# Head 0's value weights, z sums, values' ends and output blocks of a hybrid attention layer put in another order

## The chip, the cores and the metric

The kernel runs on one core of one Trainium2 chip. The metric is the device time of one execution in microseconds (us), as a median over several runs. The core has a matrix engine (TensorE, PE in the profile; its weight loads are PEld), a vector engine (DVE), an activation engine (ACT), a slower general engine (GpSimd, POOL) and a queue engine (SyncE, SP) that here issues most of the DMAs. They run side by side and wait for each other through semaphores. The profile also names SPq, the queue engine's issuing of DMAs.

## The reference

One layer of a decoder over 512 tokens plus 16 learned meta tokens, width 1024. A forgetting-attention branch (FoX, 8 heads of 128) and a matrix-memory branch (mLSTM, 4 heads, values of 512, queries and keys of 256 behind a causal convolution) run on the same normalised input, are gated and merged, and pass one output projection.

```python
h = rms_norm(x, g_pre); z = h @ w_in
(fq, fk, fv, ff, fz, mqk, mv, mi, mf, mo, mz, ga, gb) = split(z)
oa = forgetting_attention(fq, fk, fv, log_sigmoid(ff + b_fox_f))
ya = (oa * silu(fz)) @ w_a
mq, mk = split(silu(causal_conv(mqk, conv_w, conv_b)))
hb = mlstm_scan(mq * 256**-0.5, mk, mv, mi + b_i, log_sigmoid(mf + b_f))
hb = rms_norm(sigmoid(mo) * hb, g_head)      # per head
yb = (hb * silu(mz)) @ w_b
merged = sigmoid(ga) * ya + sigmoid(gb) * yb
out = x + rms_norm(merged @ w_o, g_post)     # meta tokens removed
```

All of it is float32. The kernel keeps that accuracy by splitting an operand into a high and a low part and doing three matmuls for each product (`mm3`: high x high, high x low, low x high).

## The kernel before

**Splits.** A weight chunk is loaded by SP into one of 4 raw buffers (`wload`, 512 KB), its high part is a copy on ACT, and its low part is a subtraction on DVE (`wsplit`, L142 and L144; `split`, L250 and L252). High and low parts have 4 buffers each, so a new split waits until TensorE is done with an older one.

**Products with seven multiplications.** Some projections (`mz`, `mo` of heads 1 to 3, values of heads 1 to 3, and most of the attention's) use a two by two scheme with seven block products instead of eight (`st_products`: X, Y, Z, W, Y, X, Z in that order, 12 matmuls each per unit). It needs sums of weight blocks on DVE: `st_narrow` forms them as L263, L264 (for the second and third product, s3 and s1) and L269, L270 (for the last two, s2 and s4), each followed by a split. `b` and `d` in a split's name (wz00b, wz00d) are these sums' splits, `a` and `c` the plain blocks'. The products' ends are snapshots on ACT and sums in the result's PSUM banks on DVE (L333, L334, L336).

**Order.** The four mLSTM heads come first. For each: `conv_part` for q and k (projection, then vector steps L732 to L739), values, `mo`, `score_part`, `value_part` for the chunks 3 and 2, `mz_part(h, 0)`, `value_part` for the chunks 1 and 0, `mz_part(h, 1)`. Of head 0 the values' first half is made while the input is normalised; its second half has weights of its own (`v_chunk(0, 1)`, tile wv, product pv), and its `mo` is plain (`mo_plain`, four sigmoids at L779). Heads 1 to 3 make all values in `v_seven`. Then come four pairs of attention heads; `fv_part` makes their values with `v_seven` as well, and `prob_part` the logits `pl`.

**Scores.** `score_part` takes j = 0 to 4: a product in a bank `ps`, times the decay `w` on DVE (L765), a copy to the high part `wh` on ACT (L766), the low part `wl` on DVE (L768). The last one, j = 4, is that of the meta tokens and ends with L770. `value_part` multiplies these with the values: for a chunk c and a half u (bank pnb for u = 1, pna for u = 0) three matmuls for each j (L829, L830, L831), then one with the meta rows (L832).

**Who sets the order.** The instructions stand in the program as written, each engine runs its own in a fixed order, and that order is made by the framework's scheduler when the kernel is built: it goes by program order, but lets a later instruction go ahead where, by its own model of durations, the earlier one is not ready. `pin` keeps instructions in program order, and `behind(a, b)` adds an edge so that `a` comes after `b` without a wait of its own. PSUM has 8 banks (pool `pa`), and a bank is taken again when its last reader is done. Tiles with the tag "w" share one buffer: `z` of the convolutions, the decay `w` of the scores, and `so` of heads 1 to 3.

**POOL in head 0.** The gates' rows are packed on POOL (`mr` L666, `na` L672), and behind them stands the memset of the k convolution's `z` (L708), which ACT's copies into `z` (L724) wait for.

**Output.** `wo` is taken in three parts: columns 0 to 511 with all four token blocks in four banks, and then 256 columns twice, each for the four blocks one after the other, a bank half used. A block's end is a sum of squares on ACT (L1161), a product with the gain on DVE (L1162), and after the last part the root on POOL (L1184), the two final steps (L1187) and two DMAs.

Of the kernel before, what the change touches and what calls it, by code (L numbers as in the profile page):

```python
# [10 lines left out]
BF16 = mybir.dt.bfloat16  # L11
# [42 lines left out]
def tile_hybrid_block(ctx: ExitStack, tc: tile.TileContext, x, meta, norm_pre, norm_post, w_in, b_fox_f,  # L54
# [200 lines left out]

    def st_narrow(c0, name, into=None, late=None, first=None):

        (r0,), (r1,) = (wload(win, 512 * i, 4, c0, 256, f"{name}{i}")[0] for i in range(2))
        a, b = slice(0, P), slice(P, 2 * P)
        o = {"a11": split(r0[:, :, a], f"{name}a", ("whs", "wls"), mw, 1, into)}  # L260
        if first:
            behind(split.first, first)
        V.tensor_tensor(r0[:, :, a], r0[:, :, a], r0[:, :, b], ALU.add)  # L263
        V.tensor_tensor(r0[:, :, b], r0[:, :, b], r1[:, :, b], ALU.add)  # L264
        x, y = split(r0, f"{name}b")
        o["s3"], o["s1"] = (x[:, :, a], y[:, :, a]), (x[:, :, b], y[:, :, b])
        x, y = split(r1, f"{name}c")
        o["a12"], o["a22"] = (x[:, :, a], y[:, :, a]), (x[:, :, b], y[:, :, b])
        d = V.tensor_tensor(r1[:, :, b], r0[:, :, a], r1[:, :, b], ALU.add)  # L269
        V.tensor_tensor(r1[:, :, a], r1[:, :, a], r1[:, :, b], ALU.add)  # L270
        x, y = split(r1, f"{name}d")
        if late:
            behind(d, late[0])
            behind(split.first, late[1])
        o["s4"], o["s2"] = (x[:, :, a], y[:, :, a]), (x[:, :, b], y[:, :, b])
        return o
# [17 lines left out]

    def st_products(o, units, between=lambda i: None):

# [17 lines left out]
        def halves(bank):  # L314
            return bank.rearrange("p (s n) -> p s n", s=2)
# [145 lines left out]
    def v_seven(c0, name, v, snaps, q1):  # L461
# [18 lines left out]

        st_products(o, units, meta)
        for i in (1, 0):
            for m in range(2):
                pv = units[m][i].rearrange("p (s n) -> p s n", s=2)
                hi, lo = (t[:, :, i * 256:i * 256 + 256].rearrange("p (s m) n -> p m s n", m=2)[:, m]
                          for t in (vh, vl))
                S.activation(hi, pv, AF.Copy)
                V.tensor_tensor(lo, pv, f(hi), ALU.subtract)  # L488
        v_meta(vm[:, 0:MV], pm)
# [214 lines left out]

    def conv_part(h, which):
        w = w_first[which] if h == 0 else wsplit(conv_load(h, which))
# [10 lines left out]
        for m in range(2):  # L717
            mi = which * 8 + h * 2 + m
            ps = banks(f"pqk{which}{h}{m}", 2)
            proj_t_all(ps, w, m, tz)  # L720
            y = sb([P, L], F32, "y", f"y{which}{h}{m}", bufs=2)
            for u in range(2):
                c0 = tz + u * nz
                S.activation(z[:, m, 3 + c0:3 + c0 + nz], ps[u][:, 0:nz], AF.Copy)  # L724
                S.activation(y[:, c0:c0 + nz], ps[u][:, 0:nz], AF.Identity,  # L725
                             bias=gc[:, 64 + mi:65 + mi], scale=gc[:, 48 + mi:49 + mi])
            ys.append(y)
        for m in range(2):
            mi = which * 8 + h * 2 + m
# [12 lines left out]
    def score_part(h, q, k, w):  # L742
# [10 lines left out]
        for j in range(NCH + 1):  # L753
# [13 lines left out]
            if j < NCH:  # L767
                V.tensor_tensor(wl[:, o:o + n], w[:, o:o + n], f(wh[:, o:o + n]), ALU.subtract)  # L768
            else:
                V.tensor_tensor(wh[96:128, o:o + n], w[96:128, o:o + n], f(wh[96:128, o:o + n]), ALU.subtract)  # L770
        return wh, wl
# [26 lines left out]

    def st_unit(c0, name, room, into=None, late=None, first=None):

        ps = banks(f"p{name}", 2)
        st_unit.added = st_products(st_narrow(c0, f"w{name}", into, late, first),
                                    [(ps[0], ps[1], room.rearrange("p a (b n) -> p (a b) n", b=2), None)])
# [16 lines left out]
    def value_part(h, wpk, v, so, hts, chunks):  # L820
        wh, wl = wpk
        vh, vl, vm = v
        for c in chunks:
            pn = (psum1(f"pna{h}{c}"), psum1(f"pnb{h}{c}"))
            for u in (1, 0):
                o, n = u * 256, 256 + 2 * u
                for j in range(c + 1):
# [3 lines left out]
                    T.matmul(pn[u][:, 0:n], wl[:, s0:s0 + P], vh[:, j, o:o + n], start=False, stop=False)  # L831
                T.matmul(pn[u][:, 0:n], wh[0:MP, OFFM + c * P:OFFM + (c + 1) * P], vm[0:MP, o:o + n],  # L832
                         start=False, stop=True)
            r = line(wk, f"r{h}{c}", 1, tag="r", bufs=4)
# [54 lines left out]
    for h in range(MH):  # L889
        if pend is not None:  # L890
            bt = turn_part(*pend)
        q = conv_part(h, 0)
        if h == 0:
            w1 = v_chunk(0, 1)
        k = conv_part(h, 1)
# [4 lines left out]
        if h == 0:  # L900
            v = v0
            ps = banks("pv01", 2)
            for b in range(NCH):
                proj_n(ps, w1, b)
            v_end(0, v, 1, w1, ps)
            columns()
# [264 lines left out]
    for b in range(NCH):  # L1171
        out_end(pn[b], b, 0, 512, 0)
    for u in (2, 3):
        w = wchunk(wo, 0, KC, u * 256, 256, f"wo{u}")
        for b in range(NCH):
            ps = psum1(f"pout{u}{b}")
            for k in range(KC):
                mm3(ps[:, 0:256], mh_[k // 2][:, k % 2, b * P:(b + 1) * P], ml_[k // 2][:, k % 2, b * P:(b + 1) * P],
                    w[0](k, 0, 256), w[1](k, 0, 256), k == 0, k == KC - 1)
            out_end(ps[:, 0:256], b, u * 256, 256, u - 1)  # L1180
            if u == 3:
                rs = line(wk, f"ors{b}", 1, tag="rs", bufs=7)
                V.scalar_tensor_tensor(rs, oss[:, b, 2:3], 1.0 / DM, opre[:, b:b + 1], ALU.mult, ALU.add)
                G.tensor_tensor(rs, rs, mhalf, ALU.pow)  # L1184
                for i in range(2):
                    cs = slice(i * 512, i * 512 + 512)
                    V.scalar_tensor_tensor(og[:, b, cs], og[:, b, cs], rs, xr[b][:, cs], ALU.mult, ALU.add)  # L1187
                    nc.sync.dma_start(out2[b * P:(b + 1) * P, cs], og[:, b, cs])
# [28 lines left out]
```

## Time and profile before

| | |
|---|---|
| median of 3 runs | 928.46 us (928.32 to 929.09) |
| profiled execution | 927.63 us |
| its span, first to last instruction | 925.8 us |
| TensorE busy | 906.0 us, 98% |
| vector engine busy | 730.4 us, 79% |
| activation engine busy | 504.5 us, 54% |
| POOL busy | 117.5 us, 13% |
| mean granted TensorE clock | 0.999 |

A row of the timeline gives the start in us, the length in us, the engine, the line of the kernel, the operation, what it writes and reads, the shapes and a count; in brackets stands the engine's idle time before it and what ended that. A row of the waits gives who waited for whom, the sum in us, how often, and the longest. A row of the windows gives a stretch, its length, the busy times of PE, PEld, DVE, ACT and POOL with their numbers of instructions, the granted clock, and the DMAs' share and rate. Matmuls overlap: a 512-column matmul has a length of 0.39 us in the trace, and the next one starts 0.23 us after it.

### The profile page before, as it was taken

How to read it: one execution, taken by the hardware profiler on the slowest of the kernel's cores; microseconds unless marked ns; L12 is line 12 of the kernel's file. 1: busy time of each engine (PE TensorE's matmuls, PEld its weight loads, DVE VectorE, ACT ScalarE, POOL GpSimd, SP SyncE). 2: the span in 40 equal slices, each digit the busy share in tenths (PEclk: the TensorE clock that was granted, in tenths of full speed). 3: DMA queues.
4: the chain of work that ended last, by engine and by line, in shares of the span. 5: the costliest groups of instructions: out<-in, count | busy, mean ns of one | idle time of the engine just before them, and what ended most of it. 6: DMA issues, size and time to landing. Idle time of an engine off the chain costs nothing.

```text
span 925.8 us, 16722 instructions
## 1 busy us (share of the span) xinstructions
PE 906.0 (98%) x6744; PEld 858.4 (93%) x6744; DVE 730.4 (79%) x1196; ACT 504.5 (54%) x860; POOL 117.5 (13%) x168
## 2 busy tenths in 40 slices
PE   8999899999999999999999999999999999999997
PEld 6998799899998999999999989999999999988887
DVE  6889688579887598876898866997896997985534
ACT  5646556545665456664565525565755665863231
POOL 3052000100101000000100002221333121300000
PEclk9999999999999999999999999999999999999999
DMA  7313143123331333231242442344342333258402
GB/s 233 94 50 103 46 134 91 40 69 92 117 112 57 92 91 90 95 103 51 95 114 69 124 128 73 95 123 137 100 142 81 102 112 121 87 203 300 140 18 91
DMA packets 78664, 97.54 MB, mean 105 GB/s; under 512 B 5237, under 2 KB 66773, under 8 KB 78586
## 3 DMA queue, kind: packets, MB, share of 16 engines
q1 hardware_dynamic: 76520, 92.76, 32.5%
q0 software_dynamic: 576, 2.10, 0.6%
q10 hardware_dynamic: 1490, 1.61, 0.5%
q8 instruction: 53, 0.87, 0.4%
q14 instruction: 25, 0.20, 0.1%
HBM read 90.62 MB, written 5.83 MB: 104 GB/s over the span
## 4 chain that ended last, share of the span: by engine, by line
PE 66%; DVE 22%; ACT 5%; issue 3%; DMA 2%; POOL 1%; DVEq 0%; POOLq 0%; ACTq 0%
PE pyb L151 3%; PE pyb L150 3%; PE pyb L152 3%; PE pz L150 3%; PE pz L152 3%; PE pz L151 3%; PE pqk L150 3%; PE pqk L152 3%; PE pqk L151 3%; PE pv L152 2%; PE pv L150 2%; PE pv L151 2%; PE pfk L150 2%; PE pfk L152 2%; PE pfk L151 2%
## 5 line engine op out<-in xcount | busy, mean ns | idle before, releaser
L151 PE MATMUL pyb<-bl,wb_h 128*128 128x512 f32 x128 | 49.8, 389 | 0.0
L152 PE MATMUL pyb<-bh,wb_l 128*128 128x512 f32 x128 | 49.8, 389 | 0.0
L150 PE MATMUL pyb<-bh,wb_h 128*128 128x512 f32 x128 | 49.8, 389 | 0.0
L1016 POOL TENSOR_SCALAR pn<-lt,rsum 128x128 f32<-128x128 f32 x32 | 30.4, 952 | 127.6 <-DVE rsum L1014 127.5
L732 DVE SCALAR_TENSOR_TENSOR y<-z,gc,y 128x512 f32<-128x512 f32 (+1 forms) x48 | 35.9, 754 | 2.1 <-ACT y L725 1.4
L150 PE MATMUL pfk<-hh,wfk_h 128*128 128x264 f32 x128 | 36.4, 285 | 0.0
L150 PE MATMUL pqk<-hh,wq_h 128*128 128x258 f32 x128 | 36.4, 284 | 0.0
L150 PE MATMUL pqk<-hh,wk_h 128*128 128x264 f32 x128 | 36.3, 284 | 0.0
L151 PE MATMUL pfk<-hl,wfk_h 128*128 128x264 f32 x128 | 36.3, 283 | 0.0
L152 PE MATMUL pqk<-hh,wk_l 128*128 128x264 f32 x128 | 36.3, 283 | 0.0
L152 PE MATMUL pfk<-hh,wfk_l 128*128 128x264 f32 x128 | 36.3, 283 | 0.0
L151 PE MATMUL pqk<-hl,wk_h 128*128 128x264 f32 x128 | 36.2, 283 | 0.0
L152 PE MATMUL pqk<-hh,wq_l 128*128 128x258 f32 x128 | 36.0, 282 | 0.0
L151 PE MATMUL pqk<-hl,wq_h 128*128 128x258 f32 x128 | 36.0, 282 | 0.0
L849 POOL TENSOR_TENSOR mrs<-mss,mhalf 128x1 f32<-128x1 f32 x16 | 9.2, 575 | 191.1 <-DVE mss L847 188.2
L993 POOL TENSOR_TENSOR ab<-ab,mask_q 128x128 f32<-128x128 f32 x32 | 27.0, 874 | 49.5 <-DVE vl L488 34.8
L144 DVE TENSOR_TENSOR wo_l<-wo_r,wo_h 128x1024 fp32r<-128x1024 f32 x12 | 15.7, 1313 | 16.9 <-ACT wo_h L142 16.9
L152 PEld LDWEIGHTS pyb<-bh,wb_l 128*128 128x128 f32 x128 | 24.0, 188 | 5.0
L150 PEld LDWEIGHTS pyb<-bh,wb_h 128*128 128x128 f32 x128 | 24.0, 188 | 4.9
L151 PEld LDWEIGHTS pyb<-bl,wb_h 128*128 128x128 f32 x128 | 24.0, 188 | 4.8
L884 DVE TENSOR_TENSOR yb<-pyb,yb 128x512 f32<-128x512 f32 x24 | 16.5, 686 | 13.9 <-PE pyb L152 13.9
L142 ACT ACTIVATE wo_h<-wo_r 128x1024 fp32r<-128x1024 f32 x12 | 12.7, 1059 | 24.4 <-PE pya L151 13.2
(2206 smaller groups left out, 3961.2 us busy)
## 6 DMA issues: line engine op xcount, KB each, us to landing
wv_r<-in_w_in_dram SPq DMA_DIRECT2D x16, 512.0 KB, 4.3
wo_r<-in_w_in_dram SPq DMA_DIRECT2D x16, 512.0 KB, 3.8
wz_r<-in_w_in_dram SPq DMA_DIRECT2D x16, 512.0 KB, 3.7
wb_r<-in_w_b_dram SPq DMA_DIRECT2D x16, 512.0 KB, 3.8
ab<-d_na SPq DMA_DIRECT2D x8, 672.0 KB, 4.5
wq_r<-in_w_in_dram SPq DMA_DIRECT2D x8, 512.0 KB, 3.7
wk_r<-in_w_in_dram SPq DMA_DIRECT2D x8, 512.0 KB, 3.6
wfq_r<-in_w_in_dram SPq DMA_DIRECT2D x8, 512.0 KB, 3.7
```

The lines of the kernel that those rows point to most:

```text
L142: pin(S.activation(hi, raw, AF.Copy))
L144: pin(V.tensor_tensor(lo, raw, f(hi), ALU.subtract))
L150: T.matmul(ps, ah, bh, start=start, stop=False, **kw)
L151: T.matmul(ps, ah, bl, start=False, stop=False, **kw)
L152: T.matmul(ps, al, bh, start=False, stop=stop, **kw)
L732: V.scalar_tensor_tensor(y[:, t0:L], z[:, m, t0 + j:L + j], gc[:, j * 16 + mi:j * 16 + mi + 1], y[:, t0:L], ALU.mult, ALU.add)
L849: G.tensor_tensor(rs, ss, mhalf, ALU.pow)
L884: V.tensor_tensor(dst, ps[i], dst, ALU.add)
L993: G.tensor_tensor(ab[:, o:o + P], ab[:, o:o + P], mask_q, ALU.add)
L1016: G.tensor_scalar(pn[:, o:o + P].rearrange("p (g t) -> p g t", g=4), lt[:, 0:32].unsqueeze(1).to_broadcast([P, 4, 32]), rsum, None, ALU.mult)
```

## The change

Four things are put in another order or shape; the arithmetic is the same but for the order of sums in the output's norm.

1. The load and split of head 0's second value weights stand between the q convolution's projection and its vector steps, instead of behind them.
2. In head 0 the sums L269 and L270 of `mz`'s first unit, and L263 (and so L264) of its second, come behind the last instruction of `score_part`. In chunk 3 of `value_part` both meta matmuls come after all other matmuls of the chunk.
3. `v_seven` ends a bank (copy and low part) as soon as its sums are done, instead of after all sums.
4. Columns 512 to 1023 of the output are done in one part: blocks 0 to 2 as 512-wide matmuls in a whole bank each, block 3 in two halves. In a block's last part the root's factor (`rs`) stands ahead of the product with the gain.

```diff
-    def st_narrow(c0, name, into=None, late=None, first=None):
+    def st_narrow(c0, name, into=None, late=None, first=None, sums=None):
...
-        V.tensor_tensor(r0[:, :, a], r0[:, :, a], r0[:, :, b], ALU.add)
+        d = V.tensor_tensor(r0[:, :, a], r0[:, :, a], r0[:, :, b], ALU.add)
+        if sums:
+            behind(d, sums)
...
         if late:
             behind(d, late[0])
-            behind(split.first, late[1])
+            if len(late) > 1:
+                behind(split.first, late[1])
...
-    def st_products(o, units, between=lambda i: None):
+    def st_products(o, units, between=lambda i: None, done=lambda m, i: None):
...
-        for wz, yx, snap, _ in units:
+        for m, (wz, yx, snap, _) in enumerate(units):
             V.tensor_tensor(yx[:, 256:512], snap[:, 0], yx[:, 256:512], ALU.subtract)
             V.tensor_tensor(halves(yx), halves(yx), snap[:, 2:4], ALU.subtract)
-        for wz, yx, snap, _ in units:
+            done(m, 1)
+        for m, (wz, yx, snap, _) in enumerate(units):
             last = V.tensor_tensor(halves(wz), halves(wz), snap[:, 1:3], ALU.add)
+            done(m, 0)
...
-        st_products(o, units, meta)
-        for i in (1, 0):
-            for m in range(2):
-                pv = units[m][i].rearrange("p (s n) -> p s n", s=2)
-                ...
-                S.activation(hi, pv, AF.Copy)
-                V.tensor_tensor(lo, pv, f(hi), ALU.subtract)
+        def done(m, i):
+            pv = units[m][i].rearrange("p (s n) -> p s n", s=2)
+            ...
+            S.activation(hi, pv, AF.Copy)
+            V.tensor_tensor(lo, pv, f(hi), ALU.subtract)
+
+        st_products(o, units, meta, done)
...
-    def conv_part(h, which):
+    def conv_part(h, which, between=lambda: None):
...
             ys.append(y)
+        between()
         for m in range(2):
...
-                V.tensor_tensor(wh[96:128, o:o + n], w[96:128, o:o + n], f(wh[96:128, o:o + n]), ALU.subtract)
+                score_part.last = V.tensor_tensor(wh[96:128, o:o + n], w[96:128, o:o + n], f(wh[96:128, o:o + n]),
+                                                  ALU.subtract)
...
-        ps = st_unit(C_MZ + h * MV + u * 256, f"z{h}{u}", g, into, mo_part.late if h and not u else None)
+        late = None if u else mo_part.late if h else (score_part.last,)
+        ps = st_unit(C_MZ + h * MV + u * 256, f"z{h}{u}", g, into, late, sums=None if h or not u else score_part.last)
...
+            def meta(u):
+                o, n = u * 256, 256 + 2 * u
+                T.matmul(pn[u][:, 0:n], wh[0:MP, OFFM + c * P:OFFM + (c + 1) * P], vm[0:MP, o:o + n],
+                         start=False, stop=True)
...
-                T.matmul(pn[u][:, 0:n], wh[0:MP, OFFM + c * P:OFFM + (c + 1) * P], vm[0:MP, o:o + n],
-                         start=False, stop=True)
+                if c < NCH - 1:
+                    meta(u)
+            if c == NCH - 1:
+                meta(1)
+                meta(0)
...
-        q = conv_part(h, 0)
-        if h == 0:
-            w1 = v_chunk(0, 1)
+        w1 = []
+        q = conv_part(h, 0, lambda: h or w1.append(v_chunk(0, 1)))
...
-    for u in (2, 3):
-        w = wchunk(wo, 0, KC, u * 256, 256, f"wo{u}")
-        for b in range(NCH):
-            ps = psum1(f"pout{u}{b}")
+    w = wchunk(wo, 0, KC, 512, 512, "wo_1")
+    for b in range(NCH):
+        V.tensor_scalar(opre[:, b:b + 1], oss[:, b, 0:1], 1.0 / DM, EPS, ALU.mult, ALU.add)
+        parts = [(0, 512)] if b < NCH - 1 else [(0, 256), (256, 512)]
+        for i, (c0, c1) in enumerate(parts):
+            ps = psum1(f"pout{b}{i}")[:, 0:c1 - c0]
             for k in range(KC):
-                mm3(ps[:, 0:256], ...
-            out_end(ps[:, 0:256], b, u * 256, 256, u - 1)
-            if u == 3:
+                mm3(ps, ...
+            ss = oss[:, b, i + 1:i + 2]
+            ojunk = sb([P, c1 - c0], BF16, "vm", f"ojunk{c0}{b}")
+            S.activation(ojunk, ps, AF.Square, accum_out=ss)
+            if c1 < 512:
+                V.scalar_tensor_tensor(opre[:, b:b + 1], ss, 1.0 / DM, opre[:, b:b + 1], ALU.mult, ALU.add)
+            else:
                 rs = line(wk, f"ors{b}", 1, tag="rs", bufs=7)
-                V.scalar_tensor_tensor(rs, oss[:, b, 2:3], 1.0 / DM, opre[:, b:b + 1], ALU.mult, ALU.add)
+                V.scalar_tensor_tensor(rs, ss, 1.0 / DM, opre[:, b:b + 1], ALU.mult, ALU.add)
                 G.tensor_tensor(rs, rs, mhalf, ALU.pow)
...
-            elif u == 2:
-                V.tensor_reduce(opre[:, b:b + 1], oss[:, b, 0:2], axis=mybir.AxisListType.X, op=ALU.add)
-                V.tensor_scalar(opre[:, b:b + 1], opre[:, b:b + 1], 1.0 / DM, EPS, ALU.mult, ALU.add)
+            V.tensor_tensor(og[:, b, 512 + c0:512 + c1], ps, gpost[1][:, c0:c1], ALU.mult)
+        for i in range(2):
+            cs = slice(i * 512, i * 512 + 512)
+            V.scalar_tensor_tensor(og[:, b, cs], og[:, b, cs], rs, xr[b][:, cs], ALU.mult, ALU.add)
+            nc.sync.dma_start(out2[b * P:(b + 1) * P, cs], og[:, b, cs])
```

More of the change, by code (lines that the diff above doesn't have):

```diff
@@ L479, in meta @@
                 V.tensor_tensor(pm[0:MP, 256:512], pm[0:MP, 256:512], q1[0:MP], ALU.subtract)
-        st_products(o, units, meta)
-        for i in (1, 0):
-            for m in range(2):
-                pv = units[m][i].rearrange("p (s n) -> p s n", s=2)
-                hi, lo = (t[:, :, i * 256:i * 256 + 256].rearrange("p (s m) n -> p m s n", m=2)[:, m]
-                          for t in (vh, vl))
-                S.activation(hi, pv, AF.Copy)
-                V.tensor_tensor(lo, pv, f(hi), ALU.subtract)
+        def done(m, i):
+            pv = units[m][i].rearrange("p (s n) -> p s n", s=2)
+            hi, lo = (t[:, :, i * 256:i * 256 + 256].rearrange("p (s m) n -> p m s n", m=2)[:, m]
+                      for t in (vh, vl))
+            S.activation(hi, pv, AF.Copy)
+            V.tensor_tensor(lo, pv, f(hi), ALU.subtract)
+        st_products(o, units, meta, done)
         v_meta(vm[:, 0:MV], pm)
@@ L797, in mo_part, with st_unit @@
         return so
-    def st_unit(c0, name, room, into=None, late=None, first=None):
+    def st_unit(c0, name, room, into=None, late=None, first=None, sums=None):
         ps = banks(f"p{name}", 2)
-        st_unit.added = st_products(st_narrow(c0, f"w{name}", into, late, first),
+        st_unit.added = st_products(st_narrow(c0, f"w{name}", into, late, first, sums),
                                     [(ps[0], ps[1], room.rearrange("p a (b n) -> p (a b) n", b=2), None)])
@@ L903, in tile_hybrid_block @@
             for b in range(NCH):
-                proj_n(ps, w1, b)
-            v_end(0, v, 1, w1, ps)
+                proj_n(ps, w1[0], b)
+            v_end(0, v, 1, w1[0], ps)
             columns()
@@ L1172, in tile_hybrid_block @@
         out_end(pn[b], b, 0, 512, 0)
-    for u in (2, 3):
-        w = wchunk(wo, 0, KC, u * 256, 256, f"wo{u}")
-        for b in range(NCH):
-            ps = psum1(f"pout{u}{b}")
-            for k in range(KC):
-                mm3(ps[:, 0:256], mh_[k // 2][:, k % 2, b * P:(b + 1) * P], ml_[k // 2][:, k % 2, b * P:(b + 1) * P],
-                    w[0](k, 0, 256), w[1](k, 0, 256), k == 0, k == KC - 1)
-            out_end(ps[:, 0:256], b, u * 256, 256, u - 1)
-            if u == 3:
+    w = wchunk(wo, 0, KC, 512, 512, "wo_1")
@@ new lines, in tile_hybrid_block @@
+    for b in range(NCH):
[3 more added lines that the diff above has]
+            ps = psum1(f"pout{b}{i}")[:, 0:c1 - c0]
+            for k in range(KC):
+                mm3(ps, mh_[k // 2][:, k % 2, b * P:(b + 1) * P], ml_[k // 2][:, k % 2, b * P:(b + 1) * P],
+                    w[0](k, c0, c1), w[1](k, c0, c1), k == 0, k == KC - 1)
+            ss = oss[:, b, i + 1:i + 2]
[4 more added lines that the diff above has]
+            else:
@@ L1182, in tile_hybrid_block @@
                 rs = line(wk, f"ors{b}", 1, tag="rs", bufs=7)
-                V.scalar_tensor_tensor(rs, oss[:, b, 2:3], 1.0 / DM, opre[:, b:b + 1], ALU.mult, ALU.add)
+                V.scalar_tensor_tensor(rs, ss, 1.0 / DM, opre[:, b:b + 1], ALU.mult, ALU.add)
                 G.tensor_tensor(rs, rs, mhalf, ALU.pow)
[L1185 to L1188, printed above, removed]
-            elif u == 2:
-                V.tensor_reduce(opre[:, b:b + 1], oss[:, b, 0:2], axis=mybir.AxisListType.X, op=ALU.add)
-                V.tensor_scalar(opre[:, b:b + 1], opre[:, b:b + 1], 1.0 / DM, EPS, ALU.mult, ALU.add)
+            V.tensor_tensor(og[:, b, 512 + c0:512 + c1], ps, gpost[1][:, c0:c1], ALU.mult)
```

## The prediction

> **What bounds the kernel now.** I read the waits of TensorE first, then TensorE in order of time around each of them, then the vector engine in the same stretches, because a TensorE stop is worth only what the engine it waits for can give back. The page's first line gives the span of the profiled execution:
>
> ```profile
> span 925.8 us, 16722 instructions
> ```
>
> Its own time is 927.63 us, so 1.83 us lie around the span. The median of the runs is 928.46 us, 0.83 above the profiled one; I sum against 927.63 and add 0.83 at the end. The waits of TensorE, longest first in total (us in total, times, longest):
>
> ```profile
> PE pnb L829 <- ACT wh L766: 1.8, 3, 0.7
> PE pnb L832 <- DVE wh L770: 1.7, 4, 0.6
> PE pl L150 <- DVE fvl L488: 1.6, 2, 1.4
> PE pv L151 <- DVE wv_l L144: 1.5, 1, 1.5
> ```
>
> These are exactly the waits that the edits touch: scores and z sums (L829), last chunk's meta rows (L832), the values' ends (L488), head 0's value weights (L144). The whole list is small against 925.8 us; the matmuls themselves fill the rest, and no edit removes a matmul. Now three stretches, each with the vector engine's (DVE) busy time in the third busy column:
>
> ```profile
> 66.08:96.87 30.79, 30.79 (x173) 26.60 (x172) 30.59 (x36) 20.52 (x37) 5.70 (x5) 1.00 0.34 105
> 196.03:223.30 27.27, 26.77 (x210) 25.68 (x208) 27.11 (x41) 15.62 (x25) 0.00 (x0) 1.00 0.28 79
> 588.16:625.00 36.84, 35.30 (x282) 33.78 (x282) 36.52 (x67) 22.85 (x42) 6.26 (x8) 1.00 0.30 91
> ```
>
> DVE has no free time in them: 30.59 of 30.79 us in head 0 up to the scores, 27.11 of 27.27 in head 1 from the values to the value products, 36.52 of 36.84 in the first forgetting-attention pair. There a TensorE stop is a symptom of DVE's queue. So I ask of each edit whether it takes DVE work out of the queue ahead of what TensorE waits for, or only changes the order inside it.
>
> **Head 0's value weights.** TensorE in order of time, with the idle time before the row in brackets:
>
> ```profile
> 59.60 0.38 PE L151 MATMUL pv<-wv_l,hh 128*128 128x256 f32 x1 [1.53 <-DVE wv_l L144]
> ```
>
> The second low split (`wsplit`, L144) is queued behind conv vector steps (L732, L736). `between()` puts both splits ahead of them; their inputs, the high parts on ACT, need only TensorE's q products. The 1.53 us stop goes. But the same DVE work is then done by the same time, so what comes after on DVE does not move. That matters at the scores.
>
> **Scores of head 0.** TensorE, then the last of its stops there, then DVE in the same stretch:
>
> ```profile
> 99.64 0.40 PE L152 MATMUL ps<-qkh,kr 128*128 128x512 f32 x1
> 100.66 0.39 PE L829 MATMUL pnb<-vh,wh 128*128 128x258 f32 x1 [0.62 <-ACT wh L766]
> 100.88 0.28 PE L830 MATMUL pnb<-vl,wh 128*128 128x256 f32 x1
> 101.86 0.39 PE L831 MATMUL pnb<-vh,wl 128*128 128x258 f32 x1 [0.70 <-DVE wl L768]
> 102.94 0.39 PE L829 MATMUL pnb<-vh,wh 128*128 128x258 f32 x1 [0.70 <-ACT wh L766]
> ```
>
> ```profile
> 106.12 0.38 PE L832 MATMUL pnb<-vm,wh 112*128 112x258 f32 x1 [0.65 <-DVE wh L770]
> ```
>
> ```profile
> 95.45 0.69 DVE L269 TENSOR_TENSOR wz_r<-wz_r,wz_r 128x512 f32<-128x512 f32 x1
> 96.18 0.69 DVE L270 TENSOR_TENSOR wz_r<-wz_r 128x512 f32<-128x512 f32 x1
> 98.06 1.22 DVE L252 TENSOR_TENSOR wz00d_l<-wz_r,wz00d_h 128x1024 fp32r<-128x1024 f32 x1 [1.19 <-ACT wz00d_h L250]
> 99.20 0.68 DVE L765 TENSOR_TENSOR w<-ps,w 128x512 f32<-128x512 f32 x1
> 99.98 1.23 DVE L252 TENSOR_TENSOR wz01b_l<-wz_r,wz01b_h 128x1024 fp32r<-128x1024 f32 x1
> 101.12 0.68 DVE L768 TENSOR_TENSOR wl<-w,wh 128x512 fp32r<-128x512 f32 x1
> 101.72 1.08 DVE L765 TENSOR_TENSOR w<-ps,w 128x384 f32<-128x384 f32 x3
> 102.92 1.09 DVE L768 TENSOR_TENSOR wl<-w,wh 128x384 fp32r<-128x384 f32 x3
> 103.93 0.68 DVE L765 TENSOR_TENSOR w<-ps,w 128x512 f32<-128x512 f32 x1
> 105.38 0.69 DVE L770 TENSOR_TENSOR wh<-w,wh 32x512 fp32r<-32x512 f32 x1 [0.76 <-ACT wh L766]
> ```
>
> Here the edit does take work out. `late=(score_part.last,)` moves L269, L270 and with them the split wz00d behind L770; `sums` moves the second unit's L263, L264 and its split wz01b. From 95.45 to 99.20 (3.75 us) DVE does only moved work or waits for the moved split on ACT, and wz01b_l takes 101.12 − 99.98 = 1.14 us between two score steps: 4.89 us in all. L770 ends at 106.07 now, so at 101.2 then. Is something else late there? TensorE: a stop costs its bracket and about 0.26 us more (100.88 to 101.86 is 0.98, a running pair 0.12, the bracket 0.70, so 0.16; and the matmul after a stop, 100.66 to 100.88, takes 0.22 instead of 0.12). So TensorE's scores, which end 0.23 us after 99.64, end 1.53 + 0.26 = 1.8 us earlier, at 98.1; the first L765 may start at 95.45, when its bank is full. ACT is the tighter one:
>
> ```profile
> 95.23 1.09 ACT L779 ACTIVATE yb<-po 128x512 f32<-128x512 f32 x2
> ```
>
> Four sigmoids of `mo_plain` stand ahead of wh in program order: 95.23 + 2 x 1.09 = 97.4, then wh 0.6, so the first L768 starts at about 98.0, and L768 0.6, L768 x3 1.0, L765 0.6, L770 0.7 give 100.9 to 101.3. The two accounts agree on 101.2.
>
> TensorE then starts the value products at 98.1, waits 0.3 to 1.0 us for the first wl, and has 24 matmuls of 0.12 (2.9) before the meta rows, which are now last: they come at 101.3 to 102.0, after L770, and the chunk ends 0.24 us later, at 101.5 to 102.3. Now it ends at 106.12 + 0.22 + 6 x 0.12 = 107.06. Head 0 gains 4.8 to 5.5; I take 4.7, under that end, since one score step in another place costs 0.6. Its bounds: above, all five stops, 1.53 + 0.62 + 0.70 + 0.70 + 0.65 = 4.2 plus 5 x 0.26 = 5.5; below, the first rival.
>
> The moved z work is used late: its first product s2 is the sixth of seven of 12 matmuls (1.4 us each), so 2.4 us of the next chunk and 7 us of products, 9 us, lie between, against 1.4 of sums, 1.1 of ACT and 1.2 of DVE. Its raw buffers come free later, and SP's queue waits on them:
>
> ```profile
> 96.21 3.47 SPq L129 DMA_DIRECT2D wq_r<-in_w_in_dram  x2
> ```
>
> These two loads of head 1 are issued about 6 us later, and all behind them on SP. Their user comes after 14 products of 1.4 us; I cost that at nothing, with those 20 us as the cover.
>
> **Heads 1 to 3, meta rows last.** The wait of L832 there is what is left of 1.7 us, 1.05 in three stops. What TensorE meets next, and what it waits for:
>
> ```profile
> 221.66 0.38 PE L150 MATMUL po<-wo1e_h,t4h 128*128 128x256 f32 x1 [0.15 <-ACT so L320]
> ```
>
> ```profile
> 221.03 1.07 ACT L320 ACTIVATE so<-po 128x512 f32<-128x512 f32 x2
> ```
>
> `so` shares the one buffer "w" with the scores, so L320 cannot start before L770, and L770 is the end of a DVE queue without a gap (27.11 of 27.27). Without the L832 stop TensorE reaches 221.66's matmul 0.6 us sooner and waits there 0.6 longer. I take 0. Bounds: 0 to 1.05 + 0.48 (what of L829's 1.8 us is not in head 0) + 4 x 0.26 = 2.6.
>
> **Values' ends by bank.** Same copies, same subtractions, in another order: no DVE time goes. In heads 1 to 3 nothing waits for these banks. In the attention pairs `pl` gets its bank earlier, up to 1.6 + 2 x 0.26 = 2.1 us. But TensorE's next date with DVE stays:
>
> ```profile
> 618.86 1.22 DVE L252 TENSOR_TENSOR wgb1d_l<-wgb_r,wgb1d_h 128x1024 fp32r<-128x1024 f32 x1
> ```
>
> ```profile
> 620.13 0.39 PE L152 MATMUL pgb<-t2h,wgb1d_l 128*128 128x256 f32 x1
> ```
>
> The matmul starts 0.05 us after that split ends, and DVE was busy all the way from 588.16. A TensorE that is 1.3 us earlier at 594 waits 1.3 us here. I take 0, between 0 and 2.1 on the good side; the bad side is a rival below.
>
> **Output's second half.** First matmul of the wide half, first and last of the narrow one:
>
> ```profile
> 874.56 0.39 PE L150 MATMUL pout<-wo_h,m 128*128 128x512 f32 x1
> ```
>
> ```profile
> 896.42 0.28 PE L150 MATMUL pout<-wo_h,m 128*128 128x256 f32 x1
> ```
>
> ```profile
> 919.24 0.28 PE L152 MATMUL pout<-wo_h,ml 128*128 128x256 f32 x1
> ```
>
> 96 wide ones take 21.86 us, 192 narrow ones 22.82 + 0.12 = 22.94: the same columns cost 1.08 more. Three of four blocks become wide: 0.8. The Trainium skill (TensorE: Matmul & The Clock Gate, Back-to-back issue gap) puts the isolated gap at N/2.4 + 2.5 ns, by which a wide matmul saves 2.5 ns against two narrow ones, an estimate of 0.2 us for 72 of them. This trace shows 11 ns, so the trace decides. Block 0 now needs all four splits within its own 24 matmuls:
>
> ```profile
> 898.35 1.23 DVE L144 TENSOR_TENSOR wo_l<-wo_r,wo_h 128x1024 fp32r<-128x1024 f32 x1 [0.26 <-ACT wo_h L142]
> ```
>
> The fourth ends at 899.58 and is needed 18 x 0.228 after 896.42, at 900.5: 0.9 us of cover, cost nothing. At the very end:
>
> ```profile
> 920.12 0.42 DVE L1162 TENSOR_TENSOR yb<-pout,gpost 128x256 f32<-128x256 f32 x1 [0.29 <-ACT ojunk L1161]
> 920.46 0.15 DVE L1183 SCALAR_TENSOR_TENSOR ors<-ost 128x1 f32<-128x1 f32 x1
> 921.27 1.41 DVE L1187 SCALAR_TENSOR_TENSOR yb<-yb,ors,xr 128x512 f32<-128x512 f32 x2 [0.66 <-POOL ors L1184]
> ```
>
> The new order puts `rs` ahead of the gain product, which then runs beside POOL's power: 920.46 − 920.12 = 0.34 off the tail. The eight output DMAs spread over four blocks instead of the last four quarters; the last one is as late after its vector step as now. Sum for the output: 1.15, between 0 (a stop at the fourth split eats it) and 1.4.
>
> **Sum.** 4.7 + 0 + 0 + 1.15 = 5.85 off 927.63, 921.8; with 0.83, 922.6 for the median.
>
> **The rivals.**
>
> POOL holds the head back. Behind the gates' rows on POOL stands the memset of `z` for the k convolution, which ACT's copies and then DVE from 66.08 on wait for:
>
> ```profile
> 54.15 6.47 POOL L672 TENSOR_SCALAR na<-ac 8x400 f32<-8x400 f32 x1
> ```
>
> ```profile
> 61.58 1.70 POOL L672 TENSOR_SCALAR na<-ac 8x528 f32<-8x528 f32 x1
> ```
>
> The smaller one took 6.47 us beside full-width DVE steps, the larger 1.70 beside steps on 12 rows. The change pushes 2.4 us of conv steps behind the splits, onto the larger one. At the slow rate it would take 6.47 x 528/400 = 8.5, 6.8 us more; everything DVE does up to L770 would slip by that, head 0 would lose 6.8 − 4.7 = 2.1, and the time would be 929.4. Any slip under 4.7 only shrinks the gain. Against it: DVE's work ahead of that memset is the same in sum, so its queue runs dry at the same time and lets POOL through. The Trainium skill (SBUF — State Buffer, Who interferes with whom) says that a DVE instruction with two SBUF inputs contends with a GpSimd one that reads SBUF, and the second to issue blocks. Both the moved splits and the conv steps have two such inputs, and the trace's 6.47 against 1.70 agrees with it.
>
> Slower: DVE waits at each bank's end. In `done` the subtraction follows the copy that it needs. If it is queued there, DVE stands still for the copy of 128x512, 1.07 / 2 = 0.54 us and 0.06 of hand-over, four times in each of five ends (three heads, two pairs), all on stretches where DVE bounds: 12 us, 934.6. It decides from 7.7 / 5 = 1.5 us an end on, that is when three of four copies are waited for. Against it: the framework's scheduler fills such holes with the next unit's sums, as it does now.
>
> All the stops go for good: 5.5 + 2.6 + 2.1 + 1.2 = 11.4, 917.1. It needs DVE queues that get shorter, which nothing in the diff does outside head 0.
>
> **How the numbers follow.** The forecast, 921 to 924.5 as its own range, 0.55. More than that, up to all stops, 0.12. A slip or other order that leaves 2 to 4 us of gain, 924.5 to 926.6, 0.12. No change, with the POOL slip in its full size, 0.11. Slower, the DVE waits, 0.10. About 0.2% (1.9 us) is what a measurement of this kernel tells from no change. So faster 0.79, same 0.11, slower 0.10. The range 919.0 to 928.0 leaves out half of the second case and nearly all of the slower one with a part of the fourth, some 0.2.
>
> **What would show it.** Right: no idle time before pv L151 at 59.6 and less than 1.1 us of waits before L829 to L832 in head 0, L770 near 101, L269 after it; waits of `po` on `so` in heads 1 to 3 that grow by what L832 loses; `pl` earlier but a longer wait for wgb1d_l; 512-wide `pout` rows and L1187 0.34 sooner after the last matmul. Wrong: L672 at 8 us and ACT's z copies after 66; DVE rows of L488 with an idle time from ACT before each; DVE idle in 196 to 223 or 588 to 625, which would say that its queue is not the bound; or a stop in the wide half before its sixth k.

## The result, and the profile after

The changed kernel takes 920.96 us (median of 5 runs, 920.75 to 922.35) against 928.46 (928.32 to 929.09): a ratio of 0.9921, interval 0.991 to 0.9932. The forecast was 922.6. The profiled execution took 920.75 us, 6.88 under the one of before, while the medians lie 7.5 apart; the last 0.6 us have a cause of their own, most likely the clock, on which the experiments bear.

The page's first line after, and the waits of TensorE (us in total, times, longest) that answer to the four shown of before:

```profile
span 919.0 us, 16560 instructions
```

```profile
PE pnb L835 <- DVE wh L776: 2.2, 4, 0.9
...
PE pl L150 <- DVE fvl L491: 0.8, 3, 0.3
```

The stop at the value weights and those that were put down to L829 are gone. The mask rows' wait stays (L835 is the old L832, L776 the old L770, L491 the old L488) and has grown from 1.7 to 2.2 us: the scores' waits on DVE that are left now meet in it. Head 0 in order of time, TensorE, then DVE, then POOL:

```profile
101.53 0.39 PE L835 MATMUL pnb<-vm,wh 112*128 112x258 f32 x1 [0.23 <-DVE wh L776]
101.75 0.28 PE L835 MATMUL pna<-vm,wh 112*128 112x256 f32 x1
...
104.26 0.28 PE L150 MATMUL pz<-hh,wz00a_h 128*128 128x256 f32 x1
```

```profile
100.79 0.69 DVE L776 TENSOR_TENSOR wh<-w,wh 32x512 fp32r<-32x512 f32 x1 [0.76 <-ACT wh L772]
101.50 0.69 DVE L271 TENSOR_TENSOR wz_r<-wz_r,wz_r 128x512 f32<-128x512 f32 x1
```

```profile
53.66 6.41 POOL L671 COPY mr<-ac 12x64 f32<-12x64 f32 x1
60.05 1.20 POOL L677 TENSOR_SCALAR na<-ac 8x400 f32<-8x400 f32 x1
61.20 0.31 POOL L671 COPY mr<-ac 12x64 f32<-12x64 f32 x1
61.48 1.70 POOL L677 TENSOR_SCALAR na<-ac 8x528 f32<-8x528 f32 x1
63.13 0.09 POOL L713 MEMSET z<- 128x6 f32 x1
```

DVE's last score step starts at 100.79 where it started at 105.38, the moved sums follow it, and 0.23 us of wait are left of head 0's stops. POOL's slow row is another one now, a copy of 12 rows by 64, but the 528-wide row takes its old 1.70 us and the memset of `z` has not slipped.

Where the time went, by the start of the same matmuls in both profiled executions (the difference is after minus before):

| first matmul of | before | after | difference |
|---|---|---|---|
| pz, wz00a (end of head 0's values) | 109.44 | 104.26 | -5.18 |
| pv, wv1a (head 1's values) | 178.16 | 173.30 | -4.87 |
| pz, wz31d (end of the heads) | 499.97 | 494.09 | -5.88 |
| pfv, wfv0g (first attention pair) | 589.46 | 583.57 | -5.90 |
| pga, wga3d (ahead of the output) | 827.34 | 821.52 | -5.82 |
| end of the span | 925.77 | 918.97 | -6.79 |

Head 0 gives 5.18 and loses 0.31 of it again before head 1's values, heads 1 to 3 give 1.01, the attention pairs about nothing, the output 0.97.

### The profile page after: what moved, and what is told of

Its sections match the earlier page's. It is cut to its first block, busy times and chain, and to the rows that moved or that the text cites. A ratio compares the mean times of both kernels' runs of the same rounds, so it can differ in the third digit from the quotient of the medians.

```text
span 919.0 us, 16560 instructions
## 1 busy us (share of the span) xinstructions
PE 903.3 (98%) x6672; PEld 853.9 (93%) x6672; DVE 728.8 (79%) x1190; ACT 502.1 (55%) x854; POOL 121.9 (13%) x168
## 3 DMA queue, kind: packets, MB, share of 16 engines
q10 hardware_dynamic: 1490, 1.61, 0.5%
## 4 chain that ended last, share of the span: by engine, by line
PE 66%; DVE 23%; ACT 4%; issue 4%; DMA 1%; POOL 1%; DVEq 0%; POOLq 0%; ACTq 0%
PE pyb L151 3%; PE pyb L150 3%; PE pyb L152 3%; PE pqk L150 3%; PE pqk L152 3%; PE pqk L151 3%; PE pz L150 2%; PE pz L152 2%; PE pz L151 2%; PE pv L152 2%; PE pv L150 2%; PE pv L151 2%; PE pfk L150 2%; PE pfk L152 2%; PE pfk L151 2%
## 5 line engine op out<-in xcount | busy, mean ns | idle before, releaser
L865 POOL TENSOR_TENSOR mrs<-mss,mhalf 128x1 f32<-128x1 f32 x16 | 15.2, 952 | 190.6 <-DVE mss L863 185.7
```

The lines of the kernel that those rows point to most:

```text
L865: G.tensor_tensor(rs, ss, mhalf, ALU.pow)
```

## The experiments

All shifts below are against the profiled execution of before, at the same matmuls; a minus is a gain. Medians go against the runs of before made beside them: 928.86 us beside the four runs that make one part alone in the heads (split, z sums, mask rows, values' ends), 928.69 beside the filled kernel with the split, the change without the mask rows' part and the change once more, 928.93 beside the other four.

**The value weights' split alone.**

```diff
+        between()
         for m in range(2):
...
-            w1 = v_chunk(0, 1)
+        q = conv_part(h, 0, lambda: h or w1.append(v_chunk(0, 1)))
```

> Only head 0's value weights are split ahead of the conv's vector steps; all else as before. Theory A (the vector engine's queue bounds head 0, so a TensorE stop that is taken away comes back at the next place where TensorE meets that queue): the 1.53 us stop at pv goes, the stops at the scores grow by as much, head 0 gains 0 to 0.3 us, time 928.2 to 928.5. Theory B (each stop is worth its length): 1.8 us, 926.7.

927.95 us, ratio 0.9989 (0.9979 to 0.9999). The trace is later, by 0.43 us at pz wz00a. The waits of TensorE between 57 and 130 us in it:

```profile
PE pnb L830 <- ACT wh L767: 2.2, 2, 1.7
PE pnb L832 <- DVE wl L769: 0.6, 1, 0.6
```

The stop of 1.5 us at pv is gone, and the first score stop has grown from 0.62 to 1.7: the stop moved, as the DVE queue demands. But DVE's last score step starts at 104.69, 0.69 sooner than before, and TensorE does not show it. That remained to be explained; two more runs below do it.

**The later z sums alone.**

```diff
+        late = None if u else mo_part.late if h else (score_part.last,)
+        ps = st_unit(..., into, late, sums=None if h or not u else score_part.last)
```

> Only head 0's z sums are put behind its scores. Theory A: the queue gets shorter by 4.9 us ahead of L770, so L770's counterpart ends near 101.2; TensorE still stops 1.5 us at pv, ends its scores at 99.9 and the chunk's meta rows at about 103 instead of 107.06: 4.0 us gained, 924.4. Theory B: the stops between 100 and 106, 2.67 us of idle time and 4 x 0.26: 3.7 us, 924.8. The two differ in the sum with the run before: under A the two halves together give 5.2 in the changed kernel, more than 0.2 + 4.0; under B 1.8 + 3.7 = 5.5.

924.89 us, ratio 0.9958 (0.9943 to 0.9973), -3.27 at pz, -2.77 at the end. Removing work from the queue pays alone; it pays 1.3 more when the split's move lets the queue start sooner. The 3.27 are less than either theory gave, 4.0 or 3.7: the last score step was to end near 101.2 and ended at 102.80. The first low part of the scores started at 97.89, where the prediction's account by ACT has 98.0, but 4.91 us went by from there to the end of the last step, where that account has about 3.1:

```profile
97.89 0.69 DVE L771 TENSOR_TENSOR wl<-w,wh 128x512 fp32r<-128x512 f32 x1
...
102.11 0.69 DVE L773 TENSOR_TENSOR wh<-w,wh 32x512 fp32r<-32x512 f32 x1 [0.76 <-ACT wh L769]
```

**The mask rows last, alone.**

```diff
+            if c == NCH - 1:
+                meta(1)
+                meta(0)
```

> Only the meta rows of chunk 3 come last. In heads 1 to 3 the changed kernel gained 0.3 us each (1.0 in all), which was forecast as 0. If the meta rows did that: heads 1 to 3 gain 0.9 to 1.0, head 0 up to 0.6 (five more matmuls of 0.12 ahead of the wait), 1.5 in all, 927.0. If the order of the values' ends did it: only head 0's 0.6, 927.9.

928.37 us, ratio 0.9989 (0.9978 to 1.0). The trace is again later, +0.59 at pz, and from there to the end of head 3 it falls back by 0.07 more only: nothing in heads 1 to 3, and head 0's share missing. Three stretches of head 0 in this kernel; the busy time after the stretch's length is TensorE's, and the granted clock is the third number from the end:

```profile
100.00:104.00 4.00, 1.91 (x9) 1.25 (x9) 3.88 (x9) 1.64 (x4) 0.00 (x0) 0.97 0.46 131
104.00:107.00 3.00, 3.00 (x16) 3.00 (x16) 1.30 (x3) 0.63 (x1) 0.10 (x1) 0.50 0.00 0
107.00:110.00 3.00, 3.00 (x26) 3.00 (x26) 1.98 (x9) 0.64 (x2) 0.00 (x0) 0.97 0.01 3
```

For 3 us behind the score stops the clock is 0.50, and matmuls start every 0.21 us where they start every 0.12 before and after:

```profile
104.15 0.42 PE L836 MATMUL pnb<-vh,wl 128*128 128x258 f32 x1
104.36 0.42 PE L834 MATMUL pnb<-vh,wh 128*128 128x258 f32 x1
```

The kernel before has the same stops, and its profiled execution, in the same first stretch as busy, kept its clock:

```profile
100.00:104.00 4.00, 1.90 (x10) 1.25 (x9) 3.88 (x9) 1.63 (x4) 0.00 (x0) 1.00 0.46 133
104.00:107.00 3.00, 2.35 (x20) 2.15 (x19) 1.70 (x6) 0.63 (x1) 0.10 (x1) 1.00 0.00 0
```

So a stretch in which TensorE is busy for half the time may or may not be followed by half clock. The trace with the split alone had it too, from 100.6 to 107.4 us. What differs is where the stops lie in time: in each of the 13 traces every change of the granted clock stands a whole number of steps of 3.413 us behind the trace's first. The steps ahead of 103.8 us, first in this kernel, then in the one before:

```profile
100.38:103.79 3.41, 1.65 (x7) 1.04 (x8) 3.29 (x8) 1.25 (x4) 0.00 (x0) 1.00 0.54 153
```

```profile
98.16:101.57 3.41, 2.38 (x12) 1.56 (x11) 3.31 (x4) 2.42 (x4) 0.00 (x0) 1.00 0.65 192
101.57:104.98 3.41, 2.34 (x15) 1.93 (x16) 2.93 (x8) 1.30 (x4) 0.00 (x0) 1.00 0.22 79
```

The same three stops fall into one step here, which leaves TensorE busy for 1.65 of 3.41 us, and are spread over two there. No run moved the steps against the stops, so this is a fit and not a proof.

**The same, with the stops filled.** Extra matmuls into a bank that is started anew afterwards; their results are not used.

```diff
+            def fill(j, at):
+                if h == 0 and c == NCH - 1 and u:
+                    for _ in range({(0, 0): 4, (0, 1): 5, (1, 0): 5}.get((j, at), 0)):
+                        T.matmul(pn[0][:, 0:256], vh[:, 0, 0:P], vh[:, 0, 0:256], start=True, stop=True)
```

> The kernel with the meta rows alone put last (median 928.37, granted clock mostly 0.996), and in head 0's three stops behind the scores 4, 5 and 5 extra matmuls of 256 columns (0.12 us each by the rows after it) into a bank that is started anew afterwards; nothing waits for them and the order is else the same. Theory A (the half clock from 103.9 to 107.2 us in that kernel's trace, and from 100.1 to 107.3 in the one with the value weights split early, comes from TensorE's stops there, and hides what those parts earn): granted clock 0.998 or more in nearly every run, no half-clock rows at 104 to 107 us, pz with wz00a 1.0 to 1.3 us sooner than in the trace of that kernel (110.03), median 926.7 to 927.3. Rival B (the clock falls for another reason, or the extra matmuls only lengthen the stops): median 928.1 to 928.9, half clock still there.

927.21 us (926.83 to 927.88, 11 runs), ratio 0.9982 (0.9973 to 0.9991): by the medians, 14 matmuls more make the kernel 1.2 us faster than it was without them. The granted clock was 0.998 or 0.999 in all 11 runs, where it was 0.998 in two of the ten runs without them and lower in the rest; those two took 926.7 and 926.9 us, so it is the clock that gains, and the matmuls themselves gain nothing. pz starts 0.98 sooner:

```profile
104.00:107.00 3.00, 2.95 (x24) 2.74 (x24) 1.73 (x6) 0.63 (x1) 0.11 (x1) 1.00 0.00 0
```

```profile
109.05 0.28 PE L150 MATMUL pz<-hh,wz00a_h 128*128 128x256 f32 x1
```

The stops cause the half clock here; theory A holds. Of the 59 runs of before made beside the experiments, the 8 with a mean clock of 0.999 took 927.3 to 928.3 us (mean 927.9), the other 51 had a median of 928.9.

**The filled kernel with the split moved too.**

```diff
+                    for _ in range({(0, 0): 12, (0, 1): 4, (1, 0): 3}.get((j, at), 0)):
```

> The kernel before with the value weights' split moved and the mask rows last, and 12, 4 and 3 extra matmuls in head 0's three stops behind the scores, as in the filled kernel that ran without the split's move (927.21 median, pz with wz00a at 109.04 us, subtraction of the mask row ending at 106.06 on VectorE). Theory A (the score stops end on VectorE's queue, of which the move takes only 0.7 us): subtraction at 105.3 to 105.5, pz at 108.3 to 108.5, 926.4 to 926.7. Theory B (the stop of 1.5 us ahead of pv that goes is gained whole): pz at 107.5, 925.6. With no half clock in either.

926.39 us, ratio 0.9977 (0.9967 to 0.9987); pz at 108.08, 0.97 sooner than in the filled kernel without the move, and the last score step at 104.60, also 0.97 sooner than its 105.57:

```profile
104.60 0.69 DVE L771 TENSOR_TENSOR wh<-w,wh 32x512 fp32r<-32x512 f32 x1 [0.76 <-ACT wh L767]
```

```profile
108.08 0.28 PE L150 MATMUL pz<-hh,wz00a_h 128*128 128x256 f32 x1
```

The move is worth what DVE's queue gains by it, 0.7 to 1.0 us alone and 1.3 beside the z sums, not the 1.8 that TensorE's stop suggests: nearer to A, above its figure. DVE can gain because it was not busy all the way: right ahead of the 66.08 at which the prediction's first stretch begins it stands idle, for 3.15 us before and for 2.23 with the split moved (this run):

```profile
66.08 0.69 DVE L739 TENSOR_TENSOR qkl<-y,qkh 128x512 fp32r<-128x512 f32 x1 [3.15 <-ACT qkh L738]
```

```profile
65.07 0.69 DVE L740 TENSOR_TENSOR qkl<-y,qkh 128x512 fp32r<-128x512 f32 x1 [2.23 <-ACT qkh L739]
```

**The change without the mask rows' part.**

> The changed kernel with the mask rows' matmuls where they were before (each bank's own at the bank's end). Theory A (in head 0 the one stop left is the mask row's, so moving it back brings the bank's other matmuls behind that stop; in heads 1 to 3 the gain was the values' ends' and not this part's): pz with wz00a 0.4 to 1.0 us later, heads 1 to 3 within 0.2 us, 921.4 to 922.0. Theory B (the part earns what I bounded at up to 2.6 us in heads 1 to 3): 2 to 3 us later by 500 us, 923 or more.

The edit puts `value_part` back as it was. 922.25 us, ratio 0.9929 (0.9917 to 0.9942). pz at 104.84, 0.58 later than after, and by 240 us the 0.58 is back; at the end of the heads this kernel stands at -5.95 against -5.88. So the part earns 0.58 in head 0 and gives it back in the heads behind it, more than the 0.2 us that theory A allowed there: by the traces it is worth nothing in the changed kernel as a whole. The 1.7 us by which this trace ends behind the changed kernel's arise in the attention pairs, where DVE waited 0.97 us for a load, see below.

One table settles head 0. Start of DVE's last score step, start of pz wz00a, and the difference:

| kernel | last score step | pz | between |
|---|---|---|---|
| before | 105.38 | 109.44 | 4.06 |
| z sums alone | 102.11 | 106.17 | 4.06 |
| change without mask rows' part | 100.79 | 104.84 | 4.05 |
| after | 100.79 | 104.26 | 3.47 |
| mask rows, filled | 105.57 | 109.05 | 3.48 |
| split and mask rows, filled | 104.60 | 108.08 | 3.48 |
| split alone, half clock | 104.69 | 109.87 | 5.18 |
| mask rows alone, half clock | 105.37 | 110.03 | 4.66 |
| output alone (below), half clock | 105.47 | 110.36 | 4.89 |

At full clock TensorE follows DVE's step at a fixed distance, which only the mask rows' part shortens. Half clock adds 0.8 to 1.2 us.

**The values' ends by bank, alone.**

```diff
+            done(m, 1)
...
+            done(m, 0)
```

> Only the values' ends are done by bank. Theory A: the work on the vector engine is the same, so nothing is gained in the attention pairs (pl earlier, wgb1d_l as late as before): 0 plus or minus 0.3, 928.5. Theory B: the stops at pl, 1.6 us and 2 x 0.26, are gained: 926.4. If the 0.3 us of heads 1 to 3 come from here: 927.5.

927.43 us, ratio 0.9986 (0.9977 to 0.9995). Nothing in head 0 (-0.02), -1.22 by the end of the heads, and -0.26 at the end of the span. This is where the 1.01 us of heads 1 to 3 come from. In head 1 the kernel before stops twice by its waits, 0.35 us at the mask row and 0.15 at `po` on `so`, each with its slow restart; this one stops once a head:

```profile
PE pnb L834 <- DVE wh L772: 2.3, 3, 1.0
```

From the first matmul of po with wo1a to that of pz with wz10d, the same matmuls, head 1 takes 239.49 - 206.38 = 33.11 us instead of 240.05 - 206.50 = 33.55. But merging two stops into one does not explain that. Counted by how much later matmuls start than at their running distance of 0.12 us, restarts included, the losses of this stretch are (us):

| | at the last score step, before | now | at mask row and `po`, before | now |
|---|---|---|---|---|
| head 1 | 0.30 | 0 | 1.02 | 0.95 |
| head 2 | 0.29 | 0 | 0.94 | 0.96 |
| head 3 | 0.93 | 0.34 | 0.95 | 1.24 |

The one stop costs as much as the two did. What goes is a third loss, at the products of the 128-column score step, which in heads 1 and 2 shows as no wait in the profile: there the matmuls start 0.20 to 0.23 us apart instead of 0.12. DVE's low part of that step and the matmul that uses it, before and then in this run:

```profile
218.87 0.28 DVE L768 TENSOR_TENSOR wl<-w,wh 128x128 fp32r<-128x128 f32 x1
```

```profile
219.20 0.39 PE L831 MATMUL pnb<-vh,wl 128*128 128x258 f32 x1
```

```profile
218.15 0.28 DVE L770 TENSOR_TENSOR wl<-w,wh 128x128 fp32r<-128x128 f32 x1
```

```profile
218.88 0.28 PE L833 MATMUL pnb<-vh,wl 128*128 128x258 f32 x1
```

Before, the matmul starts 0.05 us after the low part ends, so it waits for it; now the low part is done 0.45 us ahead. With the banks' ends in another order the step has come forward in DVE's queue. Behind the heads the gain is lost again in the attention pairs, whose queue opened with 0.92 us of waiting for a load in this trace:

```profile
585.50 0.69 DVE L264 TENSOR_TENSOR wfz_r<-wfz_r,wfz_r 128x512 f32<-128x512 f32 x1 [0.92 <-DMA wfz_r<-in_w_in_dram]
```

**The first z sum of the later heads behind the scores too, on the changed kernel.**

```diff
-        ps = st_unit(..., sums=None if h or not u else score_part.last)
+        ps = st_unit(..., sums=score_part.last if h or u else None)
```

> The changed kernel with the first z sum of each later head (L263, 0.69 us on VectorE, placed ahead of the mask row's subtraction L776 in heads 1 to 3) put behind that subtraction too. Theory A (L776 ends last there, and VectorE's queue ahead of it is what TensorE's one stop of 0.56 to 0.86 us per head waits for): each stop falls by 0.3 to 0.6 us, 1.0 to 1.7 us in all, 919.3 to 920.0. Rival (the z weights come late instead, since their split follows the sum): TensorE idles ahead of pz L150 in each head, and the time stays at 920.7 to 921.3 or grows.

922.88 us, ratio 0.9937 (0.9925 to 0.995), slower than the change by its trace: -4.72 at the end of the heads against -5.88. The mask rows' waits nearly go, and this comes instead:

```profile
PE po L150 <- ACT so L323: 2.6, 3, 1.0
```

```profile
215.65 0.63 ACT L250 ACTIVATE wz11a<-wz_r 128x512 fp32r<-128x512 f32 x1 [0.69 <-DMA wz_r<-in_w_in_dram]
216.19 1.07 ACT L323 ACTIVATE so<-po 128x512 f32<-128x512 f32 x2
```

`so` stands on ACT behind a split of z weights that waits for its load. The queue that the stop hangs on changed from DVE to ACT; theory A fell.

**The attention pairs: the old order of the ends there, and the change once more.**

```diff
+        if name[0] == "f":
+            st_products(o, units, meta)
+            for i in (1, 0):
+                for m in range(2):
+                    done(m, i)
```

> The changed kernel with the values' ends by bank in the heads only; in the attention pairs they stand in the old order behind all products. Theory A (in the pairs one stop is traded for several small ones, worth about nothing): within 0.3 us of the changed kernel, whose pairs moved by 0.04 us; one stop of 0.8 to 1.4 us ahead of pl in each first pair in place of five of 0.09 to 0.31. Theory B (by bank earns in the pairs what it earns in the heads, 0.4 each): 0.8 us slower than the changed kernel. Theory C (it loses there, as it did by 0.7 and 0.3 us where it was made alone): 0.5 to 1.0 us faster.

> The changed kernel once more, beside the two runs that follow. Expected 920.7 to 922.4 us as before; TensorE's landmarks within 0.1 us of the first trace up to 560 us, since all waits there end on VectorE's and ScalarE's own queues. From 560 us on theory A (the attention pairs wait for the landing of the second z weights' load ahead of L266, on which VectorE idled for 0.40 us in this kernel's trace, 0.86 and 1.09 in the two variants of it) lets the first pair differ by up to 0.7 us from the first trace, with the idle time ahead of L266 to match; theory B (it is fixed by the order of the instructions) repeats it within 0.1.

Old order in the pairs: 922.35 us, ratio 0.993 (0.9917 to 0.9942). The change again: 921.55 us, ratio 0.9924 (0.991 to 0.9938). Up to 560 us both traces repeat the first trace of the change within 0.15. In the first pair both lose about 1.4 us, in the same place. The DVE row that opens the pair's queue, in the first trace of the change and in the second, and two stretches of the second:

```profile
580.34 0.69 DVE L266 TENSOR_TENSOR wfz_r<-wfz_r,wfz_r 128x512 f32<-128x512 f32 x1 [0.40 <-DMA wfz_r<-in_w_in_dram]
```

```profile
580.86 0.69 DVE L266 TENSOR_TENSOR wfz_r<-wfz_r,wfz_r 128x512 f32<-128x512 f32 x1 [0.95 <-DMA wfz_r<-in_w_in_dram]
```

```profile
588.00:592.00 4.00, 2.70 (x15) 1.94 (x13) 3.93 (x7) 2.98 (x6) 0.00 (x0) 0.91 0.00 0
592.00:595.00 3.00, 3.00 (x16) 2.99 (x16) 2.98 (x9) 0.67 (x2) 0.00 (x0) 0.55 0.00 0
```

The second load of the z weights landed 0.52 us later, every DVE row behind it too, TensorE was busy for 2.70 of 4 us (3.12 in the first trace), and half clock followed, as it did in the three variants of the changed kernel, where DVE idled for 0.86 to 1.09 us at that load; with the values' ends alone, at 0.92, it did not. So the pair's time goes with a load's landing, and varies between executions of one kernel; why the load lands late is open. With the landing alike (0.95 and 0.86 of idle), the by-bank order (-4.53 behind the first pair) and the old one (-4.54) are equal there by the trace. Ahead of the output they stand at -4.52 and -4.23, and between the medians, 0.8 us apart with overlapping intervals, it stays open.

**The output's second half alone.**

```diff
-    for u in (2, 3):
-        w = wchunk(wo, 0, KC, u * 256, 256, f"wo{u}")
+    w = wchunk(wo, 0, KC, 512, 512, "wo_1")
```

> The kernel before with the change of the output's second half alone. My term: 1.15 us off (0.8 from 512-wide matmuls in place of two of 256, 0.34 from the shorter row of work behind the last matmul); the changed kernel's trace gained 0.97 us between its output weights and its end, so 0.97 to 1.15 is expected of the trace's end, and nothing ahead of 820 us. By the Trainium skill, TensorE: Matmul & The Clock Gate, section 'Wait — 56ns, not 53.3ns?', 2.5 ns a matmul are saved, 0.2 us by width and 0.54 in all. Rival: the gain belongs to the earlier arrival at the output and not to its shape, 0 to 0.3 us here.

927.52 us, ratio 0.9986 (0.9977 to 0.9995). Its trace had half clock at head 0 as well, so only differences count. First and last matmul of the output:

```profile
876.17 0.39 PE L150 MATMUL pout<-wo_h,m 128*128 128x512 f32 x1
...
920.16 0.28 PE L152 MATMUL pout<-wo_h,ml 128*128 128x256 f32 x1
```

43.99 us, against 919.24 - 874.56 = 44.68 before: 0.69 by width. The tail is 926.36 - 920.16 = 6.20 against 6.53: 0.33. In all 1.02, as in the changed kernel.

## Why the prediction was right, point by point

The time, 920.96, lies 1.6 us under the forecast and 0.04 under the 921 to 924.5 that the forecast had as its own. By terms, the values' ends gave 1.0 that was put at nothing, head 0 up to head 1's values 0.2 more and the output 0.2 less than its term, and 0.6 came from the step from the profiled time to the median.

- **Which waits are symptoms.** Right, and the table of head 0 is its proof: TensorE follows DVE's last score step at a fixed distance. L770 was to end near 101.2, it ended at 101.48; the z sums came behind it; chunk 3 ended at 101.87, inside 101.5 to 102.3. That L770 came out so near is in part luck. "What comes after on DVE does not move" by the split's move was wrong: DVE stood idle for 3.15 us ahead of 66.08, and the move brought its last score step 0.7 to 1.3 us forward. And the 4.89 us counted for the z sums were worth 3.27 alone. In the changed kernel the first low part of the scores started at 96.56 instead of 98.0, and from there 4.92 us went by to the end of the last step instead of some 3.1; the two errors nearly cancel.
- **Head 0, 4.7.** Measured 5.18, inside the 4.8 to 5.5 that the working gave; the deduction to 4.7 for "one score step in another place" was the error of size. 4.59 are DVE's, 0.58 the mask rows'. The 0.31 that TensorE loses again behind it, with this stop, was not foreseen. It is the mask rows' share that goes there: without their part TensorE stands at -4.60 both at pz wz00a and at head 1's values, and has no such stop:

```profile
126.73 0.52 PE L876 MATMUL pht<-ident,ht 128*128 128x128 f32 x3 [0.16 <-DVE ht L866]
```

- **Heads 1 to 3, mask rows, 0.** Not so in the changed kernel: there the part loses in these heads the 0.58 that it earns in head 0, and `po` did not come to wait for `so` more, which contradicts the sign I named for it. Right where the mask rows were moved alone: 0.07, and their stops came back as waits of `po` on `so`, as foreseen:

```profile
PE po L150 <- ACT so L320: 2.3, 3, 0.9
```

- **Values' ends, 0.** The term that failed. "Nothing waits for these banks" in the heads is not contradicted, but the order of their ends also moved the score steps on DVE, for which TensorE does wait: 1.01 us. A new order without less work was put at 0 there without a look at what else stands in the queue. In the pairs 0 held (-5.90 to -5.82), but not for the reason given: the wait for wgb1d_l did not grow; by the two traces of the change, the pair's time goes with DVE's queue from a load's landing on.
- **Output, 1.15.** 1.02: width 0.69 for 0.8, tail 0.33 for 0.34. The width's 0.8 was three of four parts of the 1.08 by which the narrow half was longer than the wide one; 0.69 came. The Trainium skill's gap (TensorE: Matmul & The Clock Gate, Back-to-back issue gap) gives 0.2, an estimate; the trace's rows were the better price.
- **The 0.83 from the profiled time to the median.** Carried over unchanged, and wrong by 0.6. The likely cause is half clock behind head 0's stops, most of which went: the traces with one step of half clock in them have mean clocks of 0.996 or 0.997, and 43 of the 59 runs of before were at 0.997 or lower. Where it stood in those runs no trace shows. After, median and profiled time are 0.21 apart; runs with a clock of 0.999 lie 927.9 - 921.2 = 6.7 apart (8 of before, 5 of the change from both of its sets), as the traces do.
- **The rivals.** POOL did not slip (1.70 us for the 528-wide row). DVE does not wait at the banks' ends: its L491 rows stand without an idle time from ACT. The stops did not all go.

## What to carry to other kernels

A stop of the bounding engine is priced by the row that ends it: find that row's queue and count the work taken out ahead of it and the idle time in it. The count is a bound and not the gain: 4.89 us were counted here, and 3.27 came. An order that takes no work away can still pay where it brings forward a step that the bounding engine waits for, and a stop costs a second time through the clock; that part shows only in the spread of the runs and in the granted clock, so compare profiled executions at equal clock before believing a difference under 1.5 us.

## What was not expected of the hardware

TensorE's clock fell to 0.50 behind stops of 0.7 us at most, when three of them left it busy for 1.91 of 4.00 us; it stayed at half for 3.4 us in that trace (103.8 to 107.2) and for 6.8 in another (100.6 to 107.4), cost 0.8 to 1.2 us at head 0, and with the same stops it did not fall in a third. Filling the stops with matmuls that nobody needs kept it at full and saved 1.2 us by the medians. The Trainium skill (TensorE: Matmul & The Clock Gate, Part 1: The HAM clock gate) has the array at half rate after an idle window of about 3.4 us, in windows that run free of the kernel. The 3.4 and 6.8 us, one and two such windows, and the steps of 3.413 us on which the clock changes in every trace agree; that a window must be idle does not, since none of these was. From what share of a window on the clock falls stays open: counted on those steps, seven windows in which TensorE was busy for 1.61 to 2.14 of 3.41 us turned the clock to half, but others of 1.76 to 2.12 did not.
